# Global attention by two key tiles at a time, maxima of two heads on the row halves of TensorE, and a reciprocal in steps

## The chip, the cores and the metric

One core of a Trainium2 chip. The metric is the device time of one launch in microseconds. A core has TensorE (matrix products into PSUM), VectorE, ScalarE and GpSimd, and 16 DMA engines; nearly all transfers are issued from SyncE's queue. In the profile they are called PE (PEld for its weight loads), DVE, ACT, POOL and SP.

## The reference

A backbone of four layers over 1024 latent and 256 context tokens of width 1024, all in fp32. Layers 0 and 3 (kind A) are grouped-query attention, layer 1 (B) is neighbourhood attention, layer 2 (C) is differential attention. Each layer is: modulated norm, one input projection (q, k, v and a gate z), mixer, gate times output projection, residual. What the change touches most is kind A:

```
logits = einsum("bqhgd,bkhd->bhgqk", qb, k) * scale      # 16 query heads, 4 key heads, 64 wide
p = softmax(logits, axis=-1)                             # latent tokens see 256 + 1024 keys
o = einsum("bhgqk,bkhd->bqhgd", p, v)
x = x + gt * ((o * silu(z)) @ w_out)
```

## The kernel before

**Products.** Most fp32 products are made from operands split into an upper and a lower part (`hi`, `lo`), as three products (two with upper parts, one with the lower). For attention, the split q and k go through DRAM. `load_k` (L569) reads k with upper and lower part stacked in 128 rows (`k1`), and once more the upper part alone with a row of ones (`k2`, 65 rows). `load_q` reads the upper part of q twice (`q1`), and the lower part (`q2`), whose 65th row later takes the negative maxima. One score tile so needs two matmuls, `k1` with `q1` and `k2` with `q2`. The value products are plain fp32, which the profile shows as two instructions for one product; the two heads of a pair write to the two column halves.

**Units.** In layers 0 and 3 the attention runs in units (`softmax_unit`, L633): two heads, 512 latent queries, ten key tiles (8 latent, 2 context); layer 0 has beside its 16 such units 8 of 256 context queries with two key tiles. A unit first needs the maximum of each query over all keys: `max_lat` and `max_ctx` compute scores with queries in the partitions (tiles `sl`, `sc`), and VectorE reduces each (`M`); `whole` merges, `rows` transposes and sends the negatives into `q2`. Then for each key tile `scores` (tile `st`), exponentials on ScalarE (`p`), the value product (`pv`, tile `o`), and an addition of `p` into one of two sums, even key tiles on GpSimd, odd ones on VectorE. At the end `finish_chunk` (L705) merges the sums, spreads them over the partitions with a product with ones (`sum`), and multiplies `o` by the gate and the reciprocal, which `inverse` (L620) makes with Ln, Exp and a correction step on GpSimd and VectorE.

**PSUM.** There are two tiles of two banks (`pa`, used for `st`) and four of one bank (`pb`, used for `sl`, `sc`, `o`, `sum`, `mT` and others).

**Order.** `unit_events` (L770) gives each step a time in key tiles, and sorts. Within that, a scheduler at compile time is free to change the order of instructions on each engine; the projections' TensorE instructions are pinned to the written order by `in_order`, those of these units are not. Events before time 0 (the first unit's loads and maxima) are spread over the steps of the last projection block. SyncE's queue issues loads in one order; a load waits there until a buffer for it is free.

**Gate blocks.** The last two blocks of each layer's projection make the gate z, 512 features each, in steps of 128 features by token group (groups of 512, 512 and 256 tokens; layer 3 needs only the first two). The tokens' `hhi`, `hlo` tiles are needed for the last time in the second of them. After the attention, `out_proj` (L837) splits the gated result tile by tile (`ogt`), multiplies with the output weights (`y`), and adds the residual.

Of the kernel before, what the change touches and what calls it, by code (L numbers as in the profile page):

```python
# [72 lines left out]
class Net:  # L73
    def __init__(self, ctx, tc, ins, out, depth):
# [6 lines left out]
        self.loads, self.order, self.pending = {}, {}, []  # L81
# [403 lines left out]
    def z_steps(self, pair, groups):  # L485
        return [lambda wop, b=b, g=g: self.proj_z_feats(wop, b, g, pair + b) for b in range(4) for g in groups]
# [133 lines left out]
    def inverse(self, s, n):  # L620

        nc = self.nc
        r = self.slot([P, n], name="r0")
        nc.scalar.activation(r, s, AF.Ln)
        nc.scalar.activation(r, r, AF.Exp, scale=-1.0)
        nc.gpsimd.tensor_tensor(s, s, r, op=ALU.mult)
        nc.vector.scalar_tensor_tensor(out=r, in0=s, scalar=-2.0, in1=r, op0=ALU.add, op1=ALU.mult)
        return r

    class Unit:  # L630
        pass

    def softmax_unit(self, qscr, heads, Ks, vsrc, og, pair, t0, n, kts, finish):  # L633
# [13 lines left out]
        def max_lat(hh, qt):  # L647
            q1 = st["q"][0]
            k1 = st["K"][hh][0][0]
            for c in range(2):  # L650
                ps = self.pb("sl")
                nc.tensor.matmul(  # L652
                    ps, q1[:, hh, qt * P : (qt + 1) * P], k1[:, c * 512 : c * 512 + 512], start=True, stop=True
                )
                nc.vector.tensor_reduce(out=st["M"][:, hh * nq + qt, c : c + 1], in_=ps, axis=AX.X, op=ALU.max)  # L655

        def max_ctx(hh, a):
            q1 = st["q"][0]
            ps = self.pb("sc").rearrange("p (q k) -> p q k", k=CTX)
            kc = st["K"][hh][1]  # L660
            for i in range(2):
                qt = a * 2 + i
                nc.tensor.matmul(ps[:, i, :], q1[:, hh, qt * P : (qt + 1) * P], kc[:, 0, :], start=True, stop=True)
            o = st["M"][:, hh * nq + a * 2 : hh * nq + a * 2 + 2, 2 if lat else 0]
            nc.vector.tensor_reduce(out=o, in_=ps, axis=AX.X, op=ALU.max)
# [34 lines left out]
        u.maxima = [lambda h=h, q=q: max_lat(h, q) for h in range(2) for q in range(nq)] if lat else []  # L700
        u.maxima += [lambda h=h, a=a: max_ctx(h, a) for h in range(2) for a in range(nq // 2)]
        u.body, u.sums, u.end = finish(st, scores, kts, n, nq, pair, t0, og)
        return u

    def finish_chunk(self, o, acc, n, t0, og, pair):  # L705

        nc = self.nc
        sp = self.pb("sum")[:, :n]
        for hh in range(2):
            nc.tensor.matmul(  # L710
                sp[hh * HD : (hh + 1) * HD, :],
                self.ones[:, :HD],
                acc[:, hh, :],
                start=True,
                stop=True,
                tile_position=(0, hh * HD),
            )
        s = self.slot([P, n], name="s")
        nc.scalar.activation(s, sp, AF.Copy)
        og = og.get(pair, t0 // 512)  # L720
        nc.vector.tensor_tensor(og, o, og, op=ALU.mult)
        r = self.inverse(s, n)
        nc.vector.scalar_tensor_tensor(out=og, in0=og, scalar=-1.0, in1=r, op0=ALU.mult, op1=ALU.mult)

    def finish_plain(self, st, scores, kts, n, nq, pair, t0, og):
        nc = self.nc
        N = len(kts)
        def pv(j, kt):
# [12 lines left out]
            side = j % 2  # L741
# [7 lines left out]
        def body(j, kt):  # L749
            scores(j, kt)  # L750
            if j > 1:
                pv(j - 2, kts[j - 2])
            if j == N - 1:
                if j > 0:
                    pv(j - 1, kts[j - 1])
                pv(j, kt)

        def sums():
            a = st["acc", 0]
            if ("acc", 1) in st:  # L760
                nc.vector.tensor_tensor(a, a, st["acc", 1], op=ALU.add)

        def end():
            self.finish_chunk(st["o"], st["acc", 0], n, t0, og, pair)

        return [lambda j=j, kt=kt: body(j, kt) for j, kt in enumerate(kts)], sums, end

    LEAD = 4

    def unit_events(self, units, extra=()):  # L770


        ev = []
        t, prev = 0.0, 8.0
        for u in units:
            n = len(u.body)
            w = max(prev, 10)
            first = t - self.LEAD - w
            ev.append((first - 6, u.load))
            for i, m in enumerate(u.maxima):  # L780
                ev.append((first + (w - 0.8) * (i + 0.5) / len(u.maxima), m))
            ev.append((t - self.LEAD - 0.8 + 0.2, u.whole))
            ev.append((t - self.LEAD + 1.5, u.rows))
            for i, b in enumerate(u.body):
                ev.append((t + i, b))
            ev.append((t + n + 0.5, u.sums))
            ev.append((t + n + 1.2, u.end))
            t, prev = t + n, n
        for lo, hi, steps in extra:
            for i, x in enumerate(steps):  # L790
                ev.append((t * (lo + (hi - lo) * (i + 0.5) / len(steps)), x))
# [900 lines left out]
```

## Time and profile before

| | |
|---|---|
| runs | 3790.03 us median of 3 (3787.66 to 3797.22) |
| profiled execution | 3785.42 us, span 3783.6 us, mean granted TensorE clock 0.985 |
| VectorE, ScalarE, GpSimd busy | 62%, 35%, 46% of the span |
| attention of layer 0 | about 358 to 908 us |
| projection, attention of layer 1 | from 1062, from 1505 us |
| attention of layer 2 | from 2368 us |
| attention of layer 3 | about 3222 to 3683 us |
| output projection of layer 3 | to the end of the span |

Times in the views are counted from the start of the span. A group of instructions is named by its line, engine and operation, with the tile written, the tiles read and their shapes. The time after a "|" or in brackets is idle time of the engine before them, with what ended it. A matmul's own duration is longer than its distance to the next one, since they are pipelined.

### The profile page before, as it was taken

To read this page: it belongs to the slowest core of one execution; us is meant where nothing else is said; L and a number is where in the kernel's file an instruction comes from. 1 tells how busy PE (TensorE), PEld (TensorE's weight loads), DVE (VectorE), ACT (ScalarE), POOL (GpSimd) and SP (SyncE) were. 2 spreads that over 40 slices of the span, in tenths; PEclk is the share of its full clock that TensorE was granted. 3 is DMA by queue.
4 is the path that set the end of the run, shared out by engine and by line. 5 is a ranking of instruction groups with operands and counts; after the bars stand their busy time and mean duration, and the time that the engine had idled before them with its cause. 6 is when DMAs were issued, how large, how long until landed. Compare 5 with 4: busy or idle time off the path is not lost.

```text
span 3783.6 us, 50547 instructions
## 1 busy us (share of the span) xinstructions
PE 3619.2 (96%) x18594; PEld 2648.8 (70%) x18594; DVE 2357.3 (62%) x3811; ACT 1333.9 (35%) x2756; POOL 1736.6 (46%) x1870
## 2 busy tenths in 40 slices
PE   7999999999999999899999999999989999999999
PEld 4887444345778888787778888888877777444447
DVE  5543666677752320888776510899986663787875
ACT  3221444343221211675122211777751221444340
POOL 5540323336642310566765510576777651334356
PEclk9999999999999999999999999999999999999999
DMA  6342442421434443553335531222113343111113
GB/s 202 80 128 78 150 128 95 139 87 56 134 91 130 121 134 81 143 150 101 119 90 139 137 117 45 80 84 85 49 43 121 103 104 91 41 36 36 42 34 89
DMA packets 229457, 370.37 MB, mean 98 GB/s; under 512 B 34088, under 2 KB 124120, under 8 KB 229212
## 3 DMA queue, kind: packets, MB, share of 16 engines
q1 hardware_dynamic: 228636, 367.01, 32.9%
q8 instruction: 147, 2.41, 0.3%
q14 instruction: 98, 0.80, 0.1%
q10 hardware_dynamic: 576, 0.15, 0.0%
HBM read 270.36 MB, written 96.57 MB: 97 GB/s over the span
## 4 chain that ended last, share of the span: by engine, by line
PE 65%; DVE 18%; POOL 8%; issue 4%; DMA 2%; ACT 2%; SPq 0%; POOLq 0%; ACTq 0%; DVEq 0%; another core or an unknown queue 0%
PE proj L382 21%; PE zT L467 11%; PE o L733 6%; PE y L873 5%; PE st L691 3%; PE sl L652 3%; PE st L692 3%; DVE ml L1424 3%; DVE p L747 2%; PE o L1094 2%; DVE wlo L133 1%; PE qkT L437 1%; POOL rstd L146 1%; PE ada L195 1%; DVE ogt L133 1%
## 5 line engine op out<-in xcount | busy, mean ns | idle before, releaser
L747 POOL TENSOR_TENSOR p<-p,p 128x1024 f32<-128x1024 f32 x128 | 317.1, 2477 | 591.6 <-ACT p L696 432.5
L382 PE MATMUL proj<-whi,hhi 128*128 128x512 f32 x1408 | 555.7, 395 | 3.7 <-POOL whi L130 2.4
L382 PE MATMUL proj<-wlo,hhi 128*128 128x512 f32 x1408 | 550.0, 391 | 3.7 <-DVE wlo L133 3.7
L382 PE MATMUL proj<-whi,hlo 128*128 128x512 f32 x1408 | 549.9, 391 | 0.0
L696 ACT ACTIVATE p<-st 128x1024 f32<-128x1024 f32 (+1 forms) x336 | 335.0, 1002 | 413.9 <-PE st L692 389.6
L655 DVE TENSOR_REDUCE M<-sl 128x1 f32<-128x512 f32 x512 | 326.9, 682 | 169.5 <-PE sl L652 168.1
L873 PE MATMUL y<-whi,ogt 128*128 128x512 f32 x1216 | 386.4, 395 | 6.9 <-POOL ogt L130 3.6
L733 PE MATMUL o<-p,v 128*64 128x512 f32 x1344 | 369.2, 609 | 1.0 <-ACT p L696 0.9
L133 DVE TENSOR_TENSOR wlo<-wraw,whi 128x1024 fp32r<-128x1024 f32 x136 | 209.7, 1555 | 197.4 <-POOL whi L130 176.3
L382 PEld LDWEIGHTS proj<-wlo,hhi 128*128 128x128 f32 x1408 | 265.4, 188 | 57.8 <-DVE wlo L133 4.9
L382 PEld LDWEIGHTS proj<-whi,hhi 128*128 128x128 f32 x1408 | 265.1, 188 | 57.7 <-POOL whi L130 2.6
L382 PEld LDWEIGHTS proj<-whi,hlo 128*128 128x128 f32 x1408 | 264.9, 188 | 55.3
L130 POOL TENSOR_SCALAR whi<-wraw 128x1024 fp32r<-128x1024 f32 x136 | 182.6, 1347 | 253.7 <-DMA wraw<-in_b_w_in_dram 86.7
L873 PEld LDWEIGHTS y<-whi,ogt 128*128 128x128 f32 x1216 | 229.7, 190 | 60.1 <-DVE ogt L133 7.3
L467 PE MATMUL zT<-hhi,whi 128*128 128x512 f32 x704 | 256.3, 364 | 6.8 <-DVE qklo L133 5.5
L467 PE MATMUL zT<-hhi,wlo 128*128 128x512 f32 x704 | 254.5, 361 | 1.3 <-DVE wlo L133 1.3
L467 PE MATMUL zT<-hlo,whi 128*128 128x512 f32 x704 | 254.7, 362 | 0.0
L747 DVE TENSOR_TENSOR p<-p,p 128x1024 f32<-128x1024 f32 x128 | 214.9, 1679 | 62.1 <-ACT p L696 61.3
L404 ACT ACTIVATE y<-proj 128x1024 f32<-128x1024 f32 (+1 forms) x68 | 65.5, 964 | 526.5 <-PE proj L382 460.2
L873 PE MATMUL y<-wlo,ogt 128*128 128x512 f32 x608 | 238.8, 393 | 0.0
L146 POOL TENSOR_TENSOR rstd<-rstd,mhalf 128x16 f32<-128x16 f32 (+3 forms) x132 | 231.2, 1751 | 10.9
L652 PE MATMUL sl<-k,q 128*128 128x512 f32 x512 | 206.6, 446 | 19.9 <-DVE M L655 14.1
(221 smaller groups left out, 7477.0 us busy)
## 6 DMA issues: line engine op xcount, KB each, us to landing
adaw<-in_ada_w_dram SPq DMA_DIRECT2D x96, 512.0 KB
xo<-xres SPq DMA_DIRECT2D x86, 256.0 KB
wraw<-in_a_w_in_dram SPq DMA_DIRECT2D x40, 512.0 KB
k<-k SPq DMA_DIRECT2D x40, 512.0 KB
q<-qkhi SPq DMA_DIRECT2D x76, 256.0 KB
q<-qklo SPq DMA_DIRECT2D x76, 256.0 KB
q<-q SPq DMA_DIRECT2D x136, 128.0 KB
wraw<-in_b_w_in_dram SPq DMA_DIRECT2D x32, 512.0 KB
```

The source lines that it names most:

```text
L130: self.nc.gpsimd.tensor_scalar(out=out, in0=in_, scalar1=1.0, scalar2=0.0, op0=ALU.mult, op1=ALU.add)
L133: self.nc.vector.tensor_tensor(out, a, b, op=ALU.subtract)
L146: nc.gpsimd.tensor_tensor(r, r, self.mhalf[:, :n], op=ALU.pow)
L382: nc.tensor.matmul(ps[:, i, :], self.h_op(a, 2 * tp + i, k), wop(b, k), start=(k == 0 and j == 0), stop=(k == KT - 1 and j == 2),)
L467: nc.tensor.matmul(ps, wop(a, k)[:, b * P : (b + 1) * P], self.h_cols(c, g, k), start=(k == 0 and j == 0), stop=(k == KT - 1 and j == 2),)
L652: nc.tensor.matmul(ps, q1[:, hh, qt * P : (qt + 1) * P], k1[:, c * 512 : c * 512 + 512], start=True, stop=True)
L655: nc.vector.tensor_reduce(out=st["M"][:, hh * nq + qt, c : c + 1], in_=ps, axis=AX.X, op=ALU.max)
L691: nc.tensor.matmul(ps[:, hh, :], self.k_op(K, 0, kt), q1[:, hh, :], start=True, stop=False)
L696: nc.scalar.activation(p, ps, AF.Exp, scale=HD**-0.5)
L733: nc.tensor.matmul(st["o"][hh * HD : (hh + 1) * HD, :], v(hh, kt), p[:, hh, :], start=j == 0, stop=j == N - 1, tile_position=(0, hh * HD),)
L747: eng.tensor_tensor(a, a, p, op=ALU.add)
L873: nc.tensor.matmul(ps, ot[a][:, k, :], wop[h](b, k), start=(k == 0 and j == 0), stop=(k == KT - 1 and j == 2))
```

## The change

The attention of layers 0 and 3 is ordered in rounds of two key tiles: both scores first, then the value products of the round before. Maxima come two steps in a round, each with one product per head, on the upper halves of the split alone (64 rows): head 0 on rows 0 to 63, head 1 on rows 64 to 127; for this k is stored with its lower part first. TensorE's instructions of these units are pinned to the written order. Additions into the sums go to GpSimd but for the last two key tiles, whose addition is on VectorE. The end of a unit becomes five steps at times of their own: `mixed` (gate product, merge of the sums), `spread` (product with ones, Ln, Exp), `error` (VectorE), `step` (ScalarE), `over` (two multiplications on GpSimd). The steps of the last unit that come after the attention (`tail`) are issued in `out_proj` behind its first products. In all layers the last gate block goes through its steps by token group. The diff, cut:

```
     def z_steps(self, pair, groups):
+        order = [(b, g) for b in range(4) for g in groups]
+        if pair == 4:
+            order.sort(key=lambda x: x[1])
+        return [lambda wop, b=b, g=g: self.proj_z_feats(wop, b, g, pair + b) for b, g in order]
...
+        def high(hh, kt):
+            rows = slice(hh * HD, hh * HD + HD)
+            K = st["K"][hh][kt][1 - hh] if kt == 0 else st["K"][hh][1][:, 1 - hh, :]
+            return K[rows], st["q"][0][rows, hh, :]
+        def max_lat(qt, c):
+            for hh in range(2):
+                k, q = high(hh, 0)
                 ps = self.pb("sl")
                 nc.tensor.matmul(
+                    ps, q[:, qt * P : (qt + 1) * P], k[:, c * 512 : c * 512 + 512], start=True, stop=True,
+                    tile_position=(hh * HD, 0),
                 )
+                st["ps", hh] = ps
+            for hh in range(2):
+                o = st["M"][:, hh * nq + qt, c : c + 1]
+                nc.vector.tensor_reduce(out=o, in_=st["ps", hh], axis=AX.X, op=ALU.max)
...
-            side = j % 2
+            side = int(j > 0 and j >= N - 2)
             eng = nc.gpsimd if side == 0 else nc.vector
...
+        def mixed():
+            nc.vector.tensor_tensor(gate, st["o"], gate, op=ALU.mult)
+            a = st["acc", 0]
+            nc.vector.tensor_tensor(a, a, st["acc", 1], op=ALU.add)
+        def spread():
+            sp = st["s"] = self.pb("sum")[:, :n]
...
+            r = st["r"] = self.slot([P, n], name="r")
+            nc.scalar.activation(r, sp, AF.Ln)
+            nc.scalar.activation(r, r, AF.Exp, scale=-1.0)
+        def error():
+            st["e"] = self.slot([P, n], name="e")
+            nc.vector.tensor_tensor(st["e"], st["s"], st["r"], op=ALU.mult)
+        def step():
+            nc.scalar.activation(st["e"], st["e"], AF.Copy, scale=-1.0, bias=2.0)
+        def over():
+            nc.gpsimd.tensor_tensor(st["r"], st["r"], st["e"], op=ALU.mult)
+            nc.gpsimd.tensor_tensor(gate, gate, st["r"], op=ALU.mult)
+        ends = [(0.47, mixed), (1.5, spread), (2.1, error), (2.2, step), (2.5, over)]
...
-    LEAD = 4
+    LEAD = 2
+    SLOTS = (0.25, 0.8)
...
+            for m in reversed(u.maxima):
+                ev.append((c + self.SLOTS[i], m))
+                c, i = (c, i - 1) if i else (c - 1, len(self.SLOTS) - 1)
...
+            for j, (a, b) in enumerate(zip(u.scores, u.products)):
+                ev.append((g + j // 2 + (0.15 if j % 2 else 0.05), a))
+                ev.append((g + j // 2 + 1 + (0.45 if j % 2 else 0.4), b))
+            ev += [(g + n + o, f) for o, f in u.ends]
...
+        pinned = lambda f: self.in_order(f, last, (self.nc.tensor.engine,))
+        ev = [(e, lambda f=f: pinned(f)) for e, f in sorted(ev, key=lambda e: e[0])]
+        self.tail = [f for e, f in ev if e >= t + 1.3]
+        return [(e, f) for e, f in ev if e < t + 1.3]
...
             products(ps, h, halves.pop(i), range(KT))
+            while self.tail:
+                self.tail.pop(0)()
...
-        kscr = self.Heads(self, "k", 4)
+        kscr = self.Heads(self, "k", 4, swap=True)
```

## Rows read from the trace of the kernel before

**Rows 1.** The page: busy time by engine, and the chain by engine.

```profile
PE 3619.2 (96%) x18594; PEld 2648.8 (70%) x18594; DVE 2357.3 (62%) x3811; ACT 1333.9 (35%) x2756; POOL 1736.6 (46%) x1870
...
PE 65%; DVE 18%; POOL 8%; issue 4%; DMA 2%; ACT 2%; SPq 0%; POOLq 0%; ACTq 0%; DVEq 0%; another core or an unknown queue 0%
```

**Rows 2.** Fourteen units of layer 3: length, busy PE PEld DVE ACT POOL, clock, DMA.

```profile
3242.45:3657.97 415.52, 400.86 (x1520) 185.74 (x1522) 333.86 (x401) 168.04 (x196) 166.24 (x78) 0.99 0.11 32
```

**Rows 3.** Groups by line and shape in the same stretch: busy, mean ns, idle before.

```profile
L747 POOL TENSOR_TENSOR p<-p,p 128x1024 f32<-128x1024 f32 x56 | 139.8, 2496 | 210.1 <-ACT p L696 198.4 <-ACT r L624 10.8 <-PE sc L663 1.0
L655 DVE TENSOR_REDUCE M<-sl 128x1 f32<-128x512 f32 x217 | 138.1, 681 | 21.4 <-PE sl L652 20.8
L747 DVE TENSOR_TENSOR p<-p,p 128x1024 f32<-128x1024 f32 x56 | 109.7, 1958 | 19.0 <-ACT p L696 18.6 <-PE o L733 0.4
L652 PE MATMUL sl<-k,q 128*128 128x512 f32 x216 | 92.8, 451 | 11.0 <-DVE M L655 11.0
...
L721 DVE TENSOR_TENSOR og<-o,og 128x512 f32<-128x512 f32 x14 | 9.5, 677 | 0.0
...
L669 DVE TENSOR_REDUCE mm<-M 128x8 f32<-128x24 f32 x14 | 2.4, 168 | 0.1
```

**Rows 4.** TensorE's timeline in one unit of layer 3: start us, us, what.

```profile
3421.11 2.80 PE L733 MATMUL o<-p,v 128*64 128x512 f32 x12
3423.84 0.73 PE L652 MATMUL sl<-k,q 128*128 128x512 f32 x2
...
3436.28 0.40 PE L691 MATMUL st<-q,k 128*128 128x512 f32 x1
...
3436.99 0.40 PE L692 MATMUL st<-q,k 65*128 65x512 f32 x1
3437.32 1.08 PE L733 MATMUL o<-p,v 128*64 128x512 f32 x4
3438.32 0.50 PE L691 MATMUL st<-q,k 128*128 128x512 f32 x1
3438.66 0.40 PE L692 MATMUL st<-q,k 65*128 65x512 f32 x1
...
3448.53 1.07 PE L733 MATMUL o<-p,v 128*64 128x512 f32 x2
```

**Rows 5.** Whole run, by tile: duration ns least/median/longest, starts, forms.

```profile
L747 POOL TENSOR_TENSOR p<-p,p x128: 2346/2378/3411, 363.6 to 3678.9; 128x1024 f32<-128x1024 f32 x128
L747 DVE TENSOR_TENSOR p<-p,p x128: 1204/1226/3409, 371.8 to 3682.9; 128x1024 f32<-128x1024 f32 x128
...
L626 POOL TENSOR_TENSOR s<-s,r x40: 724/1277/2262, 398.1 to 3689.3; 128x512 f32<-128x512 f32 x32, 128x256 f32<-128x256 f32 x8
```

**Rows 6.** Timelines of GpSimd and VectorE: two additions that meet.

```profile
3435.96 2.54 POOL L747 TENSOR_TENSOR p<-p,p 128x1024 f32<-128x1024 f32 x1 [0.42 <-ACT p L696]
...
3436.18 3.40 DVE L747 TENSOR_TENSOR p<-p,p 128x1024 f32<-128x1024 f32 x1
```

**Rows 7.** TensorE's timeline in layer 0: products on four column strips.

```profile
425.15 1.92 PE L195 MATMUL ada<-adaw,cT 128*32 128x512 f32 x16
```

**Rows 8.** TensorE's timeline at the ends of both attentions: the last sums.

```profile
908.74 0.61 PE L710 MATMUL sum<-p,ones 128*64 128x512 f32 x1 [2.14 <-DVE p L761]
...
3686.19 1.08 PE L710 MATMUL sum<-p,ones 128*64 128x512 f32 x4 [3.64 <-DVE p L761]
```

**Rows 9.** Layer 1: SyncE's queue and VectorE by time, then engines' busy time.

```profile
1467.19 0.36 SPq L123 DMA_DIRECT2D q<-q  x1
1493.02 0.32 SPq L123 DMA_DIRECT2D k<-k  x1
...
1504.83 0.39 SPq L123 DMA_DIRECT2D raw<-in_pen_dram  x1
...
1521.88 1.29 DVE L1036 CAST k<-raw 58x1024 fp32r<-58x1024 f32 x2 [6.42 <-DMA raw<-in_pen_dram]
...
1505.00:1525.00 20.00, 9.23 (x62) 7.31 (x60) 10.91 (x32) 8.51 (x27) 3.31 (x8) 0.71 0.76 185
```

More of the change, by code (lines that the diff above doesn't have):

```diff
@@ L80, in __init__ @@
         self.n = 0
-        self.loads, self.order, self.pending = {}, {}, []
+        self.loads, self.order, self.pending, self.tail = {}, {}, [], []
         self.consts()
@@ L485, in z_steps @@
     def z_steps(self, pair, groups):
-        return [lambda wop, b=b, g=g: self.proj_z_feats(wop, b, g, pair + b) for b in range(4) for g in groups]
+        order = [(b, g) for b in range(4) for g in groups]
+        if pair == 4:
+            order.sort(key=lambda x: x[1])
+        return [lambda wop, b=b, g=g: self.proj_z_feats(wop, b, g, pair + b) for b, g in order]
     def project_attend(self, w, blocks, events, cut):
@@ L618, in get @@
             return self.block(pair // 2, g)[:, pair % 2, :]
[L620 to L628, printed above, removed]
     class Unit:
@@ L699, in softmax_unit, with finish_plain @@
         u.load, u.whole, u.rows = load, whole, rows
-        u.maxima = [lambda h=h, q=q: max_lat(h, q) for h in range(2) for q in range(nq)] if lat else []
-        u.maxima += [lambda h=h, a=a: max_ctx(h, a) for h in range(2) for a in range(nq // 2)]
-        u.body, u.sums, u.end = finish(st, scores, kts, n, nq, pair, t0, og)
-        return u
[L705 to L725, printed above, removed]
+        u.maxima = [lambda q=q, c=c: max_lat(q, c) for q in range(nq) for c in range(2) if lat]
+        u.maxima += [lambda a=a: max_ctx(a) for a in range(nq // 2)]
+        u.scores = [lambda j=j, kt=kt: scores(j, kt) for j, kt in enumerate(kts)]
+        u.products, u.ends = finish(st, kts, n, pair, t0, og)
+        return u
+    def finish_plain(self, st, kts, n, pair, t0, og):
         nc = self.nc
@@ L747, in pv @@
                 eng.tensor_tensor(a, a, p, op=ALU.add)
[L749 to L758, printed above, removed]
-            a = st["acc", 0]
[L760 to L764, printed above, removed]
@@ L766, in finish_plain @@
-        return [lambda j=j, kt=kt: body(j, kt) for j, kt in enumerate(kts)], sums, end
-    LEAD = 4
+        gate = og.get(pair, t0 // 512)
+        def mixed():
+            nc.vector.tensor_tensor(gate, st["o"], gate, op=ALU.mult)
+            a = st["acc", 0]
+            nc.vector.tensor_tensor(a, a, st["acc", 1], op=ALU.add)
+        def spread():
+            sp = st["s"] = self.pb("sum")[:, :n]
+            for hh in range(2):
+                nc.tensor.matmul(
+                    sp[hh * HD : (hh + 1) * HD, :],
+                    self.ones[:, :HD],
+                    st["acc", 0][:, hh, :],
+                    start=True,
+                    stop=True,
+                    tile_position=(0, hh * HD),
+                )
+            r = st["r"] = self.slot([P, n], name="r")
+            nc.scalar.activation(r, sp, AF.Ln)
+            nc.scalar.activation(r, r, AF.Exp, scale=-1.0)
@@ L770, in unit_events @@
+        return [lambda j=j, kt=kt: pv(j, kt) for j, kt in enumerate(kts)], ends
+    LEAD = 2
+    SLOTS = (0.25, 0.8)
     def unit_events(self, units, extra=()):
+        starts, t = [], 0
+        for u in units:
+            starts.append(t)
+            t += len(u.scores) // 2
         ev = []
[L774 to L788, printed above, removed]
+        c, i = t, 0
+        for u, g in reversed(list(zip(units, starts))):
+            if c >= g - self.LEAD:
+                c, i = g - self.LEAD - 1, len(self.SLOTS) - 1
+            for m in reversed(u.maxima):
+                ev.append((c + self.SLOTS[i], m))
+                c, i = (c, i - 1) if i else (c - 1, len(self.SLOTS) - 1)
+            ev.append((min(c, g - self.LEAD - 6) - 1.5, u.load))
+            n = len(u.scores) // 2
+            ev.append((g - self.LEAD - 1 + 0.9, u.whole))
+            ev.append((g - self.LEAD + 0.17, u.rows))
+            for j, (a, b) in enumerate(zip(u.scores, u.products)):
+                ev.append((g + j // 2 + (0.15 if j % 2 else 0.05), a))
+                ev.append((g + j // 2 + 1 + (0.45 if j % 2 else 0.4), b))
+            ev += [(g + n + o, f) for o, f in u.ends]
@@ L789, in unit_events @@
         for lo, hi, steps in extra:
             for i, x in enumerate(steps):
-                ev.append((t * (lo + (hi - lo) * (i + 0.5) / len(steps)), x))
-        return sorted(ev, key=lambda e: e[0])
+                e = t * (lo + (hi - lo) * (i + 0.5) / len(steps))
+                ev.append((math.floor(e) + 0.6 + (e % 1) / 10, x))
+        last = {}
+        pinned = lambda f: self.in_order(f, last, (self.nc.tensor.engine,))
+        ev = [(e, lambda f=f: pinned(f)) for e, f in sorted(ev, key=lambda e: e[0])]
```

24 lines of the change are left out of this document (11 added, 13 removed).

## The prediction

> **What bounds the kernel now.** I read the page first: TensorE holds 96% of the span, and the chain that ended last is mostly its [rows 1]. A busy TensorE is not yet TensorE at its peak, so I went to the stretch that the change touches, the global attention of layer 3, and took fourteen units between two equal marks: 415.52 us, 29.68 us for a unit (one head pair, 512 queries, ten key tiles). VectorE is busy 333.86 us of it, 23.85 us a unit; ScalarE and GpSimd are busy under half of it [rows 2].
>
> What does TensorE need for a unit? Starts in its timeline give the price of one matmul of 512 columns: scores follow each other by 0.234 us (3436.28 to 3436.99 is three), twelve value products take 2.73 us, 0.2275 each [rows 4]. A change between the whole array and column halves costs about 0.1 us each way: the value products come 0.33 us after the last score instead of 0.234, and the first score after them is followed at 0.34 us [rows 4]. A unit has 40 scores (9.36 us), 40 value products (9.1), 16 maximum products (3.74), 8 of 256 columns (half as long, 0.94), four sum products (0.91), a small transpose (taken as 0.1, an estimate from 128 columns against 512) and, in the unit that starts at 3421, ten runs of column halves, of which the first and the last are shown (2.0): 26.15 us. So 3.5 us of the 29.68 are waits. Whose? The maximum products sit idle for VectorE's reduction, 11.0 us in the stretch [rows 3], and VectorE is late because it does 20 reductions of 0.68 us and accumulates every second key tile, at 1.96 us a time [rows 3]. That addition takes 1.2 us alone and 3.4 us at worst [rows 5]; in the timeline the 3.40 us one ends 1.1 us after GpSimd's own addition did, so it stood until GpSimd was through [rows 6]. Attention, then, is bound by TensorE with VectorE close behind it and feeding waits into it.
>
> **The change, part by part.**
>
> *Additions.* Seven of eight additions go to GpSimd (four before), one stays on VectorE (four before). GpSimd: 7 x 2.496 = 17.5 us, and two multiplications over 512 columns at the 1.28 us median [rows 5] 2.6: 20.1 us a unit. VectorE: 20 x 0.682 = 13.6 (the number of reductions stays), one addition at up to 3.4, the merge 1.23 (the same operation as the addition, at its median), gate product 0.68, the new error product 0.68 (nearest row: the gate product, which also reads one operand from PSUM), the small maximum 0.17: 19.8 us against 23.85 [rows 2, 3, 5]. ScalarE trades a copy for the correction step: no change, and it is idle more than half the time [rows 2].
>
> The Trainium skill, page "SBUF — State Buffer", section "Who interferes with whom", speaks against part of this: a VectorE instruction with two SBUF inputs stands until a GpSimd instruction that reads SBUF is done, and the reverse. The 3.40 us row agrees. By that rule only the two additions can still collide, since gate and error product read one operand from PSUM, and the 19.8 us above already holds one collision.
>
> *Maxima.* The scores for the maxima use only the upper half of the split, 64 contraction rows, so that the two heads are set on the two row halves. The trace has no row halves; bounds come from column strips. Sixteen products on four strips took 1.92 us, 0.12 each [rows 7], against 0.2275 on two strips [rows 4]: strips do run beside each other there. If row halves do the same, a pair costs 0.234 us, and 16 products 1.9 us; if they go one after the other, 0.468 and 3.74. I take the first, because the strips are the nearest thing; the 256-column ones I leave at 0.94, since each brings a weight load of its own.
>
> The Trainium skill, page "TensorEngine Tiling (Array Packing)", section "Key Properties", says that changing the tiling mode drains the array. The 0.1 us above is that drain as the trace shows it. By the rule the new order is dearer: a round of two key tiles goes whole, rows, columns, rows, whole.
>
> *Order.* Five rounds of four changes make 2.0 us, about 0.1 more for the transpose. TensorE's order is now fixed as written. Its sum: 9.36 + 9.1 + 1.9 + 0.94 + 0.91 + 0.1 + 2.1 = 24.4 us (26.3 if the halves run one after the other), against 26.15.
>
> *What waits next.* A pair of maxima takes two of the four small PSUM banks at once, one is held by the value product, so a pair needs the reductions of the pair before. Behind a late VectorE instruction stand the next reductions, and behind these TensorE, now with nothing to move ahead. The late one will be the merge: it needs GpSimd's seventh addition. GpSimd gets two additions (4.99 us) in a round of about 5.2 us, and the two multiplications of the unit before (2.6 us) fall in the middle, so the seventh comes 1 to 3 us behind its place, against a slack of some 2 us between two pairs. I put the leftover waits at 2.0 us a unit, between 0.7 (the small transpose alone, which follows its reductions directly) and the 3.5 of now. Unit: 24.4 + 2.0 = 26.4 us. There are 32 such units in layers 0 and 3 (the eight context units, two key tiles each, I cost at no change): 32 x (29.68 - 26.4) = -105 us.
>
> *Tail.* The last unit's sums, reciprocal and gating are issued after the first output products. Today TensorE stands 3.64 us before that sum in layer 3 and 2.14 us in layer 0, with output products ready behind it [rows 8]. The first output tiles don't need that unit's tokens, so these waits go: -3.6 and -2.1, -6 together; bounds 0 and -12 (twice as much, if the last units before that sum are also straightened).
>
> *Last gate block by groups.* It frees token group 0 after four of twelve steps instead of ten. In layer B the loads of the first heads wait for just this: the queue stands from 1467 to 1493, then issues all at once, and the mask for the second window table is only issued at 1504.83 [rows 9]. VectorE stands on that mask for 6.42 us, and in the 20 us after the projection TensorE is busy 9.23 us at a mean clock of 0.71 [rows 9]. With loads some 20 us earlier I take -9 us, bounds 0 and -11. For layers A and C I take nothing (bounds 0 and -5 together). The other order of k in memory issues the same transfers.
>
> **Sum.** -105 - 6 - 9 = -120 us. The profiled execution took 3785.4 us (its span is 3783.6); that becomes 3665. The median shown is 3790.0, 4.6 above the profiled one, so the time to expect of a median is 3670; the rivals below start from the median too.
>
> **The rivals.**
>
> *Row halves run one after the other.* For: no row of the trace shows them. Against: the four strips. The unit is 26.3 + 2.0 = 28.3 us, -44, with the edges (-15) -59: 3731.
>
> *The waits nearly vanish.* For: VectorE drops to 19.8 us and its long collisions go. Against: fixed order and the merge. 24.4 + 0.7 = 25.1 us, -147, edges -15: 3628.
>
> *Slower: GpSimd becomes the bound.* Place: the chain of seven additions. Its longest addition was 3.41 us, its longest multiplication 2.26 [rows 5]; at those prices 7 x 3.41 + 2 x 2.26 = 28.4 us, plus the two VectorE additions of 1.2 us for which it stands, 30.8 us a unit: +36, edges -15: 3811. It decides from a mean addition of about 3.3 us on. Against it: the mean is 2.496 while VectorE adds four times as often [rows 3]. The skill's page "SBUF — State Buffer", in the section named, gives the rule by which each addition on one engine would stop the other.
>
> *No change.* The fixed order gives back what VectorE wins: pairs that each wait 0.45 us, ten a unit, bring 24.4 + 4.5 + 0.7 = 29.6 us, -3 in all, and with edges of -6 (their bounds are 0 and -28) 3781.
>
> **How the numbers follow.** Forecast 0.50, row halves one after the other 0.22, waits gone 0.14, no change 0.05, GpSimd the bound 0.09. Within 0.3% (11 us) is what a measurement of this kernel can't tell from no change. Faster: 0.50 + 0.22 + 0.14 = 0.86; same 0.05; slower 0.09. The range goes from 3605 (a unit of 25.1 us with the lower bounds of the edges, 3785 - 147 - 28 = 3610, and a little less) to 3750 (halves one after the other with 2.7 us of waits).
>
> **What would show it.** Marks between units 26.4 us apart in layer 3; the two maximum products of a pair starting within 0.05 us of each other (or 0.23, if they go one after the other); VectorE under 20 us a unit, GpSimd near 20; waits of TensorE for the maxima halved; output products starting right after the last value products; the pen mask issued before 1500 in layer B's equivalent place and no 6 us of VectorE on it. The prediction is wrong if GpSimd's additions are back to back over the whole unit, or if TensorE stands at every pair.

## The result, and the profile after

The changed kernel takes 3667.89 us in the median of four runs (3665.29 to 3671.03); the kernel before, run beside it, 3793.62 (3787.66 to 3799.44). The ratio is 0.9669, 95% interval [0.965, 0.9688]. The forecast was 3670. That the sum came out is in part luck: the units gained more than forecast, the ends of the attentions lost what they were to gain, and the two errors cancelled. One of the four runs of `alt_adds` below took 4324.43 us at a granted clock of 0.748, and its ratio leaves that run out.

The page of the changed kernel, to be held against [rows 1]: busy time by engine, then the chain by engine. TensorE works 101 us less with as many instructions; VectorE falls from 2357 to 2154 us, GpSimd rises from 1737 to 1999.

```profile
PE 3518.5 (96%) x18594; PEld 2615.8 (71%) x18594; DVE 2153.7 (59%) x3675; ACT 1323.0 (36%) x2756; POOL 1998.8 (54%) x2006
...
PE 68%; DVE 16%; POOL 9%; issue 4%; DMA 2%; ACT 1%; SPq 0%; POOLq 0%; ACTq 0%; DVEq 0%
```

Where the span's 114.4 us went (3783.6 to 3669.2), from the marks of the two traces (end of the last gate block, first output product):

| stage | before | after |
|---|---|---|
| attention of layer 0, to the first output product | 558.4 | 503.1 |
| attention of layer 1 | 273.0 | 264.4 |
| attention of layer 3, to the first output product | 470.1 | 413.4 |
| output projection of layer 3 | 96.4 | 100.9 |
| all other stages together | 2385.7 | 2387.4 |

Eleven units of layer 3, columns as in [rows 2]. The marks (the first value product of each unit) stand 25.07 to 25.09 us apart; before, from one run of twelve value products to the next, it was 28.2 to 31.6, 29.68 in the mean. TensorE is busy 275.59 of 275.90 us. VectorE does 16.35 us a unit, GpSimd 19.4.

```profile
3186.90:3462.80 275.90, 275.59 (x1199) 132.86 (x1199) 179.84 (x276) 129.78 (x155) 213.72 (x105) 1.00 0.15 43
```

The groups of that stretch that answer to [rows 3]. TensorE no longer stands before the maximum products (0.0, before 11.0), while VectorE now stands for them (77.8). VectorE's addition (L739) and its merge (L747) take 1216 ns each: neither meets a GpSimd addition, where before the mean was 1958.

```profile
L739 POOL TENSOR_TENSOR p<-p,p 128x1024 f32<-128x1024 f32 x77 | 182.7, 2373 | 62.6 <-PE o L725 58.3
L660 DVE TENSOR_REDUCE M<-sl 128x1 f32<-128x512 f32 x177 | 113.0, 685 | 77.8 <-PE sl L653 77.8
L653 PE MATMUL sl<-k,q 64*128 64x512 f32 x176 | 44.2, 497 | 0.0
...
L774 POOL TENSOR_TENSOR r<-r,e 128x512 f32<-128x512 f32 x11 | 14.1, 1283 | 0.0
L775 POOL TENSOR_TENSOR og<-og,r 128x512 f32<-128x512 f32 x11 | 14.1, 1279 | 0.9
L747 DVE TENSOR_TENSOR p<-p,p 128x1024 f32<-128x1024 f32 x11 | 13.4, 1216 | 0.0
L739 DVE TENSOR_TENSOR p<-p,p 128x1024 f32<-128x1024 f32 x11 | 13.4, 1216 | 0.0
```

One round on TensorE, against [rows 4]. From one run of value products to the next it is 4.81 us: eight in 1.87, a pair of maxima on either side of the eight scores (0.43 and 0.44 to what follows).

```profile
3302.59 1.94 PE L725 MATMUL o<-p,v 128*64 128x512 f32 x8
3304.46 0.50 PE L653 MATMUL sl<-k,q 64*128 64x512 f32 x2
3304.89 0.50 PE L700 MATMUL st<-q,k 128*128 128x512 f32 x1
3305.23 0.40 PE L701 MATMUL st<-q,k 65*128 65x512 f32 x1
...
3306.64 0.39 PE L701 MATMUL st<-q,k 65*128 65x512 f32 x1
3306.96 0.51 PE L653 MATMUL sl<-k,q 64*128 64x512 f32 x2
3307.40 1.94 PE L725 MATMUL o<-p,v 128*64 128x512 f32 x8
```

At the ends of both attentions there are new waits. In layer 0 the last sums now stand 9.43 us (before 2.14 [rows 8]); in layer 3 a maximum waits 3.33 us, and the first output product 7.83 us for GpSimd's rounding of the gated result. The first three rows are TensorE's; the fourth is VectorE behind the second, held by GpSimd; the last two are GpSimd's queue ahead of the third. GpSimd comes out of the attention with additions still to do.

```profile
855.63 1.97 PE L753 MATMUL sum<-p,ones 128*64 128x512 f32 x4 [9.43 <-DVE p L747]
...
3508.93 0.79 PE L653 MATMUL sl<-k,q 64*128 64x512 f32 x1 [3.33 <-DVE M L660]
...
3568.28 0.79 PE L897 MATMUL y<-whi,ogt 128*128 128x512 f32 x1 [7.83 <-POOL ogt L130]
...
3504.92 3.35 DVE L133 TENSOR_TENSOR wlo<-wraw,whi 128x1024 fp32r<-128x1024 f32 x1 [2.79 <-POOL whi L130]
...
3562.24 5.62 POOL L739 TENSOR_TENSOR p<-p,p 128x1024 f32<-128x1024 f32 x2
3567.82 1.84 POOL L130 TENSOR_SCALAR ogt<-og 128x256 fp32r<-128x256 f32 x4
```

Layer 1, against [rows 9]: the loads of the first heads begin to be issued at 1413.56, 36 us ahead of the gate block's end (1449.6), where before they came 12 us ahead. The mask (second row, SyncE's queue) is issued at 1447.50, only 2 us ahead, but VectorE's cast of it at 1458.52 has no wait before it (before 6.42 us [rows 9]). In the 20 us after the gate block TensorE is busy 17.13 us at a clock of 0.91 (before 9.23 at 0.71).

```profile
1413.56 0.32 SPq L123 DMA_DIRECT2D k<-k  x1
...
1447.50 0.27 SPq L123 DMA_DIRECT2D raw<-in_pen_dram  x1
...
1458.52 1.30 DVE L1062 CAST k<-raw 58x1024 fp32r<-58x1024 f32 x2
```

```profile
1449.00:1469.00 20.00, 17.13 (x139) 14.02 (x137) 17.60 (x56) 13.92 (x45) 8.53 (x17) 0.91 0.72 189
```

### The profile page after: what moved, and what is told of

It reads as the page before. It is cut to its first block, busy times and chain, and to the rows that moved or that the text cites. A ratio compares the mean times of both kernels' runs of the same rounds, so it can differ in the third digit from the quotient of the medians.

```text
span 3669.2 us, 50527 instructions
## 1 busy us (share of the span) xinstructions
PE 3518.5 (96%) x18594; PEld 2615.8 (71%) x18594; DVE 2153.7 (59%) x3675; ACT 1323.0 (36%) x2756; POOL 1998.8 (54%) x2006
## 4 chain that ended last, share of the span: by engine, by line
PE 68%; DVE 16%; POOL 9%; issue 4%; DMA 2%; ACT 1%; SPq 0%; POOLq 0%; ACTq 0%; DVEq 0%
PE proj L382 21%; PE zT L467 11%; PE o L725 8%; PE y L897 6%; PE st L700 5%; PE st L701 4%; PE sl L653 3%; DVE ml L1450 3%; PE o L1120 2%; POOL rstd L146 2%; DVE wlo L133 2%; DVE ogt L133 1%; PE qkT L437 1%; POOL hhi L130 1%; POOL p L739 1%
## 5 line engine op out<-in xcount | busy, mean ns | idle before, releaser
L739 POOL TENSOR_TENSOR p<-p,p 128x1024 f32<-128x1024 f32 x224 | 540.1, 2411 | 326.1 <-PE o L725 287.4
L705 ACT ACTIVATE p<-st 128x1024 f32<-128x1024 f32 (+1 forms) x336 | 324.4, 1003 | 314.8 <-PE st L701 303.1
L725 PE MATMUL o<-p,v 128*64 128x512 f32 x1344 | 324.5, 605 | 1.7 <-DVE M L660 1.1
L467 PE MATMUL zT<-hhi,whi 128*128 128x512 f32 (+1 forms) x704 | 256.6, 365 | 5.9 <-DVE qklo L133 5.6
L467 PE MATMUL zT<-hhi,wlo 128*128 128x512 f32 (+1 forms) x704 | 254.3, 361 | 1.3 <-DVE wlo L133 1.3
L467 PE MATMUL zT<-hlo,whi 128*128 128x512 f32 (+1 forms) x704 | 254.2, 361 | 0.0
L700 PE MATMUL st<-q,k 128*128 128x512 f32 x512 | 218.3, 426 | 2.3 <-ACT p L705 2.3
L410 DVE TENSOR_TENSOR y<-y,rstd 128x1024 f32<-128x1024 f32 (+1 forms) x68 | 104.1, 1531 | 193.0 <-POOL rstd L146 193.0
```

The lines of the kernel that those rows point to most:

```text
L467: nc.tensor.matmul(ps, wop(a, k)[:, b * P : (b + 1) * P], self.h_cols(c, g, k), start=(k == 0 and j == 0), stop=(k == KT - 1 and j == 2),)
L700: nc.tensor.matmul(ps[:, hh, :], self.k_op(K, 0, kt), q1[:, hh, :], start=True, stop=False)
L705: nc.scalar.activation(p, ps, AF.Exp, scale=HD**-0.5)
L725: nc.tensor.matmul(st["o"][hh * HD : (hh + 1) * HD, :], v(hh, kt), p[:, hh, :], start=j == 0, stop=j == N - 1, tile_position=(0, hh * HD),)
L739: eng.tensor_tensor(a, a, p, op=ALU.add)
```

## The experiments

Question: which part took 4.6 us from each unit? Theory 1: VectorE lost three of four additions. Theory 2: the row halves. Theory 3: TensorE's pinned order. After these fell, theory 4 (the reciprocal in steps), 5 (the order by rounds), 6 (several of these, each enough). All ratios are to the kernel before.

**Additions by turns** (`alt_adds`).

```
-            side = int(j > 0 and j >= N - 2)
+            side = j % 2
```

> The changed kernel with the additions of p alternating between GpSimd and VectorE again, as before the change; all else as changed. Theory 1 (the units got faster because VectorE lost three of its four additions, so its reductions are no longer late): the waits of TensorE for the maxima come back; a unit in the even part of layer 3's attention takes 27.5 us or more instead of 25.08, VectorE about 21 to 24 us of it, and the run ends at 3735 us or later (25.08 to 27.5 is 2.4 us, 32 units, 77 us). Theory 2 (the row halves made TensorE's own work shorter) and theory 3 (the fixed order by rounds of two key tiles): a unit stays within 25.1 to 25.8 us, the run within 3665 to 3695.

Measured: 3681.08 us, 0.9705 [0.9686, 0.9725], 13 us more than the changed kernel. The unit takes 25.67 us with VectorE busy 22.5 (thirteen units in the row). Theory 1 as the only cause falls.

```profile
3202.64:3536.30 333.66, 328.26 (x1407) 158.83 (x1407) 293.07 (x364) 152.87 (x181) 175.40 (x86) 1.00 0.14 41
```

**Maxima on all 128 rows** (`full_rows`): `high` returns `k1` and the doubled q whole, without `tile_position`.

> The changed kernel with the products for the maxima on all 128 rows, one head after the other, with upper and lower part of k, as before; order, additions and reciprocal as changed. Theory 2: most of the 4.6 us of a unit is lost, a unit takes 28 us or more, the run 3760. Theory 1 and 3: a pair costs 0.47 us instead of about 0.33, and two changes of the array's shape in a round go away: a unit of 25.0 to 26.2 us, the run 3665 to 3705.

Measured: 3667.36 us, 0.9671 [0.9656, 0.9685]: no difference. The unit is 25.32 us, so the row halves are worth 0.24 us each, and the ends give that back (the last three intervals of layer 3 take 84.3 us together, in the changed kernel 86.7). Theory 2 falls. One round, to be held against the round of the changed kernel above: 4.86 us from one run of value products to the next, where that one takes 4.81.

```profile
3303.75 0.40 PE L698 MATMUL st<-q,k 65*128 65x512 f32 x1
3303.99 0.63 PE L652 MATMUL sl<-k,q 128*128 128x512 f32 x2
3304.55 1.94 PE L722 MATMUL o<-p,v 128*64 128x512 f32 x8
3306.41 0.72 PE L652 MATMUL sl<-k,q 128*128 128x512 f32 x2
3306.98 0.40 PE L697 MATMUL st<-q,k 128*128 128x512 f32 x1
3307.21 0.40 PE L698 MATMUL st<-q,k 65*128 65x512 f32 x1
```

**TensorE's order free** (`free_order`): the events are sorted, but not passed through `in_order`.

> The changed kernel with TensorE's instructions of the attention units not pinned to the written order, so that the scheduler may move them; additions, row halves and reciprocal as changed. Theory 3: the units lose the rhythm and most of the gain, a unit varies and takes 28 us or more, the run 3750 or later. Theory 1: VectorE still has 16.4 us of work in a unit and is on time in most orders: a unit of 25 to 26.5 us, the run 3660 to 3715.

Measured: 3707.28 us, 0.9774 [0.976, 0.9789], 39 us more. In layer 3 the unit stays at 25.2 us. About 30 us are lost in layer 0 (533.4 us to the first output product, 503.1 with the pin, 558.4 before), where TensorE is as full (98.6 of the 100 us from 700, 98.63 with the pin) but gets 439 matmuls through where the pinned one does 474, and single-head runs of two value products appear. So theory 3 is no cause of the gain of layer 3's unit, but more than half of layer 0's gain hangs on the pin; why the compiler's order is bad in layer 0 alone wasn't followed further.

**The kernel before, with seven additions on GpSimd** (`before_adds`), the reverse of the first edit.

> The kernel before with one edit only: the additions of p go to GpSimd but for the last two key tiles. Theory 1: VectorE falls from 23.9 to about 18 us a unit and its waits go: a unit of 26.2 to 27.5 us instead of 29.68, the run about 3700 to 3735. Theory 2 and 3: the unit stays at 29 us or more, the run above 3765. A third way: without the reciprocal in steps, GpSimd's part of the reciprocal stands behind seven additions in one queue and VectorE waits for it, so that nothing is gained or the run is slower than before.

Measured: 3845.29 us, 1.0142 [1.0127, 1.0157], slower by 52. The view of VectorE's waits over nine units (engine, line, what it waited for: us in total, times, longest) shows VectorE standing 23.3 us for GpSimd's product in the reciprocal, which is queued behind additions:

```profile
DVE M L655 <- PE sl L652: 34.4, 23, 3.2
DVE r L627 <- POOL s L626: 23.3, 9, 3.3
```

Before, with as many additions on VectorE as on GpSimd (56 and 56 in [rows 3]), the same wait was 10.5 us in fourteen units:

```profile
DVE r L627 <- POOL s L626: 10.5, 10, 1.2
```

The move of additions is a loss by itself; it needs another part of the change.

**The last gate block by features** (`feature_order`): the sort in `z_steps` is left out.

> The changed kernel with the last gate block in the order by features again in all layers. If the order by token group is what took 8.6 us out of layer 1 (from the last gate product to the first output product 273.0 us before, 264.4 after), that stretch is back at 271 to 275 us, VectorE stands for the second table's mask for some 6 us, and the run is 6 to 12 us later than the changed kernel's 3668. If the 8.6 us came with the earlier start of the layer's other loads, or by chance, the stretch stays at 264 to 266 us.

Measured: 3677.68 us, 0.9697 [0.9683, 0.9712], 9.8 us more; layer 1's attention is back at 274 us, and the 20 us after its gate block again show TensorE busy for under half:

```profile
1449.00:1469.00 20.00, 9.17 (x58) 7.54 (x58) 10.28 (x31) 8.52 (x27) 2.98 (x7) 0.77 0.74 183
```

So the group order is the cause of layer 1's 8.6 us.

**No tail** (`no_tail`): `unit_events` returns all events, and `out_proj` finds none.

> The changed kernel with the last unit's sums, reciprocal and gating issued at the end of the attention, not behind the first output products. If the tail is worth what the prediction gave it, the run is about 6 us later. If GpSimd's queue (the last additions, weight splits and the first splits of the gated tokens) sets the start of the output products now, the sums cost TensorE nothing that it doesn't wait anyway: the run stays within 4 us of 3668 and the last value products to the first output product in layer 3 take 7 to 9 us as they do now (7.83 us of waiting).

Measured: 3665.04 us, 0.9667 [0.9651, 0.9683]: the tail is worth nothing. In layer 3 the sums stand 13.8 us for VectorE's merge; with the tail the wait sits at the first output product instead. The two views of TensorE's waits, layer 3's end without the tail, then with it:

```profile
PE sum L753 <- DVE p L747: 14.7, 2, 13.8
```

```profile
PE y L897 <- POOL ogt L130: 9.1, 3, 7.8
```

**Additions by turns in the last two units alone** (`end_alt`), to take GpSimd's backlog away where it shows.

```
+                self.alt = g == 3 and t0 == 512
...
+            side = j % 2 if alt else int(j > 0 and j >= N - 2)
```

> The changed kernel with the additions of the last two latent units of layers 0 and 3 alternating between GpSimd and VectorE; the other 28 units as changed. If GpSimd's backlog of additions is what holds up the end of both attentions (TensorE stands 9.43 us before the last sums of layer 0 and 7.83 us before the first output product of layer 3), these two waits fall below 3 us each and the run is 8 to 16 us faster than the changed kernel, about 3655. If the splits themselves or the loads are late, the waits stay and the run is at 3664 to 3672.

Measured: 3651.95 us, 0.963 [0.9615, 0.9645], 16 us under the changed kernel. The sums of layer 0 now stand 0.4 us (9.43), the output products of layer 3 at most 2.8 (7.83).

**The same, and the first output weights rounded on ScalarE** in layers 0 and 3 (`end_alt_act`).

```
-            self.round_pool(parts[a][0], raw[a])
+            (rnd or self.round_pool)(parts[a][0], raw[a])
```

> As the run before it, and the upper halves of the first output weight block of layers 0 and 3 are rounded on ScalarE instead of GpSimd. In the changed kernel VectorE stands for GpSimd's rounding and then shares its port in the last units of layer 3, and TensorE stands 3.33 us for VectorE (at 3505 us). If that is a cost of GpSimd's queue, that wait goes too: 3 to 8 us faster than the run with the alternating end alone, about 3648 to 3652. If it is VectorE's subtraction that is in the way, no change.

Measured: 3643.96 us, 0.961 [0.9595, 0.9624], 24 us under the changed kernel and the fastest of all; the 3.33 us wait is gone too. These two show that the waits at the ends were GpSimd's backlog: with work taken off GpSimd there, they go.

**The reciprocal in one piece** (`old_recip`).

```
-        ends = [(0.47, mixed), (1.5, spread), (2.1, error), (2.2, step), (2.5, over)]
+        ends = [(0.47, mixed), (1.5, spread)]
...
+            nc.scalar.activation(s, sp, AF.Copy)
+            nc.scalar.activation(r, s, AF.Ln)
+            nc.scalar.activation(r, r, AF.Exp, scale=-1.0)
+            nc.gpsimd.tensor_tensor(s, s, r, op=ALU.mult)
+            nc.vector.scalar_tensor_tensor(out=r, in0=s, scalar=-2.0, in1=r, op0=ALU.add, op1=ALU.mult)
+            nc.vector.scalar_tensor_tensor(out=gate, in0=gate, scalar=-1.0, in1=r, op0=ALU.mult, op1=ALU.mult)
```

> The changed kernel, with the reciprocal of before in one piece: copy, logarithm and exponential on ScalarE, one product on GpSimd, two fused products on VectorE, all issued at the place of the sum product; additions, row halves, order as changed. Theory 4 (VectorE no longer stands in its queue for GpSimd in the middle of the reciprocal; that alone took 3 to 4 us from each unit): the unit goes from 25.1 to about 28 to 29 us, 3760 to 3790 us in all, with VectorE seen waiting for GpSimd at its fused product. Theory 5 (the order by rounds of two key tiles, with the maxima set between the rounds, is what takes the waits away): under 3685 us, unit under 25.7. Theory 6 (each of several measures leaves enough slack, so that no one of them undone brings the waits back): 3670 to 3710.

Measured: 3918.27 us, 1.0332 [1.0316, 1.0348]: 250 us more than the changed kernel, well past any expectation, and slower than before. The unit is 35.2 us. Over eleven units VectorE stands 58.8 us for GpSimd's product; behind it stand the reductions, behind these TensorE (72 of 387 us), and the granted clock goes to and fro between 2.4 and 1.2 GHz (0.86 in the mean). First the window, then the wait:

```profile
3307.28:3694.39 387.11, 314.91 (x1200) 148.30 (x1200) 227.84 (x287) 130.35 (x154) 202.94 (x95) 0.86 0.11 31
```

```profile
DVE r L767 <- POOL e L766: 58.8, 11, 5.7
```

**The order by rounds alone** (`order_only`): additions by turns, maxima on all rows and the reciprocal in one piece, all three from above.

> The changed kernel with additions by turns, maxima on all 128 rows and the reciprocal of before in one piece: of the change to the global attention only the order by rounds and the pinning of TensorE to it are left (the group order in the last gate block and the tail stay as changed). Theory 5 (the order alone): at most 3690 us, unit 25.1 to 25.7. Theory 4 (the reciprocal): as with the reciprocal undone alone, 3760 to 3790. Theory 6 (several measures, each enough): clearly more than the sum of the single losses, that is over 3720, while each alone costs under 40.

Measured: 3772.00 us, 0.9949 [0.9932, 0.9965]; less layer 1's part there is some 12 us left of gain, and layer 3's unit is longer than before, 30.9 us. VectorE, busy 276 of 340 us and held 0.85 us a unit by GpSimd, is what TensorE waits for: the small transpose and the context maxima stand 34.6 us for it, all of TensorE's idle time in the stretch; the clock is 0.92 in the mean. First the window of eleven units, then waits of TensorE and of VectorE in it:

```profile
3252.43:3592.59 340.16, 305.60 (x1195) 159.98 (x1194) 276.18 (x318) 129.11 (x154) 121.50 (x59) 0.92 0.13 38
```

```profile
PE mT L683 <- DVE mm L675: 22.4, 11, 5.2
PE sc L666 <- DVE M L671: 12.2, 8, 1.6
...
DVE r L764 <- POOL e L763: 9.3, 11, 2.3
```

Theory 5 in its form "the order alone" falls; theory 4's 3760 to 3790 and theory 6's "over 3720" both hold here.

**The kernel before, with the reciprocal in steps** (`before_recip`): `finish_chunk` ends after Exp; the error product, the correction and the two GpSimd products follow 1.2, 1.4 and 2.0 key tiles later.

> The kernel before, with the reciprocal in steps: the error product from PSUM on VectorE, correction on ScalarE, two products on GpSimd, set 1.2, 1.4 and 2.0 key tiles behind the sum product; additions by turns, maxima on all rows, order as before. Theory 4: the unit goes from 29.7 to about 26, 3680 us. Theory 5: within 20 us of before (3770 to 3795), because the waits of the maxima for VectorE stay where they are. Theory 6: a gain of 40 to 110 us.

Measured: 3753.16 us, 0.9898 [0.9883, 0.9913], 40 us under before: theory 6's lower edge, a third of theory 4's gain. The unit takes 28.36 us, and TensorE is busy for all but 1.3 us of ten units:

```profile
3238.55:3522.14 283.59, 282.28 (x1092) 133.22 (x1090) 224.52 (x281) 119.98 (x142) 133.01 (x65) 1.00 0.13 37
```

```profile
3186.23:3490.08 303.85, 303.85 (x1309) 168.04 (x1309) 197.16 (x301) 141.57 (x168) 233.20 (x115) 1.00 0.16 45
```

This is the reading that settles the unit. With the waits nearly gone, the old order still needs 28.2 us of TensorE, the order by rounds with the same products 25.32 (`full_rows`, twelve units in the second row). What is in the 28.2 shows in its timeline: value products in runs of four, and once a unit a maximum product of the next unit falls between the two heads of one key tile. Each head's run of two then takes 1.00 us, as long as both heads' run of four together (1.01):

```profile
3418.02 1.08 PE L745 MATMUL o<-p,v 128*64 128x512 f32 x4
3419.03 0.74 PE L652 MATMUL sl<-k,q 128*128 128x512 f32 x2
...
3423.75 1.07 PE L745 MATMUL o<-p,v 128*64 128x512 f32 x2
3424.75 0.49 PE L652 MATMUL sl<-k,q 128*128 128x512 f32 x1
3425.18 1.07 PE L745 MATMUL o<-p,v 128*64 128x512 f32 x2
3426.18 0.50 PE L652 MATMUL sl<-k,q 128*128 128x512 f32 x1
```

**Value products in runs of four** (`split_runs`), to price a change between the whole array and column halves.

```
-                ev.append((g + j // 2 + 1 + (0.45 if j % 2 else 0.4), b))
+                ev.append((g + j // 2 + 1 + (0.45 if j % 2 else 0.1), b))
```

> The changed kernel, with one thing in the written order altered: in each round of two key tiles the value products of the first tile stand between the scores of the two tiles of the round, and not beside the value products of the second. So a unit has ten runs of four products on column halves (and one with the sums) in place of five runs of eight; nothing is added and nothing removed. Theory 5a (the order by rounds gained by having fewer changes between the whole array and the halves, about 0.1 us each): ten changes more, 1.0 us a unit, the unit from 25.08 to about 26.1, the kernel from 3668 to about 3700 (3690 to 3710). Theory 5b (the order gained by slack for the maxima and their reductions, and the number of changes does not matter): unit 25.0 to 25.3, under 3676. Over 3720 would mean that the place of the value products matters for another reason (a wait for the exponentials or for a bank).

Measured: 3716.51 us, 0.9804 [0.9787, 0.982], 48.6 us more. The mechanism of theory 5a holds (TensorE is busy for the whole stretch, no wait for anything), its price was too low: the unit is 26.75 us, each of eleven in the first row like the others, 1.67 more for five runs more, so 0.33 us for a change there and back. The timeline has the three pieces: the last score before the run is followed at 0.33 (0.234 among scores), the run of four at 1.01 (0.91 for four at 0.2275), the first score behind it at 0.34:

```profile
3212.49:3506.77 294.28, 294.28 (x1201) 123.28 (x1199) 182.13 (x275) 133.31 (x155) 213.66 (x106) 1.00 0.14 41
```

```profile
3301.03 0.40 PE L701 MATMUL st<-q,k 65*128 65x512 f32 x1
3301.36 1.08 PE L725 MATMUL o<-p,v 128*64 128x512 f32 x4
3302.37 0.50 PE L700 MATMUL st<-q,k 128*128 128x512 f32 x1
3302.71 0.39 PE L701 MATMUL st<-q,k 65*128 65x512 f32 x1
```

The mean unit of layer 3 in one table (maxima on all rows in the first four lines, on row halves in the last three):

| order | reciprocal | additions | unit, us |
|---|---|---|---|
| by key tile | one piece | by turns | 29.68 (before) |
| by key tile | one piece | seven on GpSimd | 31.1 |
| by key tile | steps | by turns | 28.36 |
| rounds | one piece | by turns | 30.9 |
| rounds | one piece | seven on GpSimd | 35.2 |
| rounds | steps | by turns | 25.67 |
| rounds | steps | seven on GpSimd | 25.08 (changed) |

With additions by turns, the order by rounds alone costs 1.2 us, the steps alone gain 1.3, and both together gain 4.0 (some 0.24 of it by the row halves). That is neither one cause nor, as theory 6 had it, several each of which is enough: each needs the other. The rounds take 2.9 us from TensorE's own work, but alone they leave TensorE standing for VectorE (3.1 us a unit in `order_only`) at a lower clock; the steps take the stand for GpSimd out of VectorE's queue. The additions come third: +1.4 and +4.3 us on GpSimd with the reciprocal in one piece, -0.6 with the steps. The eighth case, the order by key tile with steps and seven additions on GpSimd, was not run.

## Why the prediction was right, and where not

*TensorE's own time of a unit* was put at 26.15 us before and 24.4 after. It was 28.2 (`before_recip`, the old order with hardly a wait) and 25.1. The step that failed is "five rounds of four changes make 2.0 us", set against ten runs of column halves at 2.0: by it the order saved nothing. A run there and back costs 0.33, not 0.2, and ten runs became five (the sums follow a run of value products now): 1.7 us. The two heads of a key tile that the old order tore apart cost another 0.9. Together 2.6 of the 2.9 us by which `before_recip` and `full_rows` differ; 0.3 I can't place. For a round of the changed kernel, its changes to row halves included, the term was too small as well: 4.81 us less eight scores, eight value products and two pairs at the forecast's prices (4.16) leaves 0.65, where 0.4 was put.

*The row halves* were taken at 0.234 us a pair, 1.8 us a unit gained. The halves do run beside each other, as forecast: 176 products of 497 ns each keep TensorE busy for only 44.2 us, 0.50 a pair, and the two of a pair start 0.003 to 0.004 us apart. But a pair and its change take 0.43 to 0.44 us against 0.56 to 0.57 on all rows, and the scores next to it pay for the change too: the pair comes 0.32 us after the last score (0.24 on all rows), and the first score behind a pair is followed at 0.34 (0.23). What is left is 0.05 us a round and 0.24 us a unit. The step that failed here is that the price of a pair stood at 0.234 us, with the changes around it only in the 2.0. The rival "row halves one after the other" had the wrong mechanism and nearly the right effect.

*Waits* were put at 3.5 before and 2.0 after. They were 1.0 to 1.5 and none: [rows 2] has TensorE idle for 14.66 of 415.52 us, 1.05 a unit (1.5 is 29.68 less 28.2), so the 3.5 that the sum left over could have been seen to be too much, and the products' own time too little. In the two stretches TensorE's busy time falls from 28.63 to 25.05 us a unit and its idle time from 1.05 to 0.03: of the 4.6 us gained, 3.6 are the products' own time and 1.0 are waits. The merge that I had expected late meets no GpSimd addition: both VectorE additions of a unit take 1216 ns. GpSimd's time was right (20.1 forecast, 19.4), VectorE's too high (19.8 forecast, 16.35), 2.2 of it for the collision that didn't come. Such collisions there are at the attention's end: VectorE's split of an output weight takes 3.35 us at 3504.92, beside a GpSimd addition that starts at 3504.85 and ends 1.1 us before the split does, and 1.21 at 856.34, with GpSimd idle. The Trainium skill, page "SBUF — State Buffer", section "Who interferes with whom", has the rule (a VectorE instruction with two SBUF inputs contends with a GpSimd instruction that reads SBUF, and the later one stands until the other is done); this trace agrees.

So the unit fell by 4.6 us where 3.3 was forecast, close to the rival "the waits nearly vanish" (25.1 us), which I gave 0.14 and whose term for TensorE's own was as wrong as the forecast's. 32 units would then give 147 us; the two attentions gave 112. Forecast were 105 and 6 for the tail, 111: the 42 us that the units gave beyond the forecast are nearly the 35 that were lost elsewhere and the 6 of the tail. That these cancel is luck; no step of the prediction has the surplus or the loss.

*Tail.* Forecast -6, worth nothing (`no_tail`). The place was right, but I had counted today's waits and not what the new split of additions leaves at the end: GpSimd is behind there by a part of its 19.4 us, because the rounding of output weights and of the gated result is queued with the additions on the same engine. The last three intervals of layer 3 are 33.16, 23.09 and 30.44 us, 11.5 more than three steady units. `end_alt` and `end_alt_act` get 24 us back. Not all of the 35 us between 147 and 112 is shown: the units of layer 0 run beside other products and weren't taken apart.

*Group order.* Forecast -9, measured -8.6, and +9.8 when undone. That the mask would be issued before the equivalent of 1500 was wrong: it is issued 2 us ahead of the gate block's end, where before it was 1 us. What is earlier are the loads in front of it, now spread over 36 us; that the mask lands sooner because they no longer come at once is the likely reason, and not shown.

*GpSimd as the bound*: `before_adds` and `old_recip` are slower than before, as that rival said, but by another mechanism than mine. The additions stayed at 2.4 to 2.5 us, GpSimd was busy 18.4 of 35.2 us a unit in `old_recip`, and VectorE stood in its queue for a GpSimd product behind them. I had named the mean addition as what decides; it is the wait in the middle of VectorE's queue.

## What to carry to other kernels

Before an engine is given more of a shared sum, take away the places where another engine stands in its queue for it: here the same move cost 52 us in the old order without that step, some 146 in the order by rounds without it (`old_recip` against `order_only`, which differ in the row halves too), and gained 13 with it. Where TensorE is full, count how often products on the halves and on the whole array follow each other, and read the price from three distances (into the run, the run, out of it); making the runs twice as long took more from this kernel than running two products beside each other. An engine that is off the path in the steady stretch can be on it at the end of the stage, where its backlog has to be worked off: look at the last two units by themselves.

## What the runs showed of the hardware

- A change from the whole array to column halves and back took 0.33 us in `split_runs` (1.67 us for five, at a granted clock of 1.00).
- Two value products of one head alone took as long (1.00 us) as four of both heads (1.01).
- In `old_recip`, where TensorE stands 72 of 387 us for VectorE, the granted clock falls to 1.2 GHz again and again (0.86 in the mean), and TensorE takes 28.6 us of busy time a unit for the same products that the changed kernel does in 25.05 at 1.00: the unit there is longer by the waits and by slower products.
